# The reload of x for the residual, held behind the attention projection's sixth finished tile on GpSimd's own queue

## Chip, cores and metric

The kernel runs on one core of one Trainium2 chip. The metric is the device time of one execution in microseconds (us). "Median" is the median over the timed runs. The profile comes from one further execution; its span runs from the first to the last instruction, and its own device time is a little longer than its span.

## What is computed

One step of a hybrid decoder layer on 512 prompt tokens and 8 x 8 sample tokens (576 columns in all), with a model width of 1024. The part around the change is the end of the attention branch, the merge of the two branches by their gates, the output projection and the gated residual:

```python
mod = jax.nn.silu(c) @ w_ada + b_ada
sh1, sc1, g1, sh2, sc2, g2 = [m[:, None, :] for m in jnp.split(mod, 6, axis=-1)]
h = _rmsnorm(x, norm1_g) * (1.0 + sc1) + sh1
...
ya = (b_gate * uc) @ w_conv_out
...
yb = o @ w_attn_out
mixed = jax.nn.sigmoid(ga) * ya + jax.nn.sigmoid(gb) * yb
x = x + g1 * (mixed @ w_mix_out)
h2 = _rmsnorm(x, norm2_g) * (1.0 + sc2) + sh2
a, val = jnp.split(h2 @ w_up, 2, axis=-1)
```

After that come the FFN with its depthwise convolution, a second residual and a final norm.

## The kernel before

Activations are held transposed, as tiles of 128 features x 576 tokens; a matrix of width 1024 therefore is eight tiles (`NK = 8`). Every fp32 operand is split into a high and a low part (`split`, L136), and a product is three matmuls for each pair of tiles: high by high, high by low, low by high (`kstep`, L203; `product`, L215). ScalarE (ACT) makes the high parts, VectorE (DVE) the low parts. Some low parts of weights are made by a DMA that adds into its target, issued by GpSimd (POOL) in L175 and L408 (`wlo<-raw`, `wl<-s`).

SyncE (SP) issues nearly all loads: weight blocks of 512 KB into four buffers (`load_w`, L146, tile `raw`), columns of `w_ada` in pieces of 256 KB (L1234, tile `ada`), and the gates that had been parked in DRAM (`gate`, L1346, tile `gt`, 288 KB).

The modulation `mod` is made in the background. `modulation` (L1225) is a generator that loads 32 `ada` pieces and after every eight of them puts a group of 16 small matmuls on TensorE (PE), `side_by_side` (L1213, matmuls at L1218). `tick` (L188) pulls it along by a rate for each `kstep`. The last modulation (`modulations(1)`, L1472) runs beside the attention projection and gives the scale and gate of the FFN's norm and residual, so it has four such groups. What is left of it is run by `drain()` (L1522).

The loop at L1487 is the attention projection, `yb`. It goes through the eight output tiles in the order `turn = [0, 4, 1, 5, 2, 6, 3, 7]`; for the n-th tile it makes the product with `w_attn_out`, multiplies by the gate and adds `ya` (L1503, L1504). The result `t` is tile m = turn[n] of `mixed`, which is then split (L1513); for m >= 4, pair sums for the next product are made from it (L1521). The sixth finished tile is n = 5.

x had been written to a DRAM tensor `xT_dram` early in the kernel (L801). L1553 to L1556 read it back, as two transfers of 1152 KB on GpSimd's queue, into two buffers of the tag "oh", which held the attention output `ot` until then. The first reader is the residual after the first product with `w_mix_out` (L1590).

The order within each engine is set in two ways. Engines named in `pinned` keep the order of the program text; PE, ACT and DVE are pinned up to the fourth product of the loop (`pinned.clear()`, L1499) and again from L1589. Everything else is ordered by the compiler's planner, which runs a timeline of its own (`schedule_with_timeline_sim`, L2077). `tc.issue_after(i)` keeps the instructions traced inside its block behind instruction `i` where they are on the engine of `i`; it adds no wait between engines.

```python
        done = dve.tensor_tensor(out=t, in0=t, in1=ya[m], op=ALU.add)
        if n == 4:
            x1_after = done
...
    x1t = [wp.tile([P, 4, NT], F32, tag="oh", name=nm("x1"), bufs=2) for _ in range(2)]
    with tc.issue_after(x1_after.ins):
        for x in range(2):
            nc.gpsimd.dma_start(x1t[x], xT_dram[x])
```

Of the kernel before, what the change touches and what calls it, by code (L numbers as in the profile page):

```python
# [10 lines left out]
F32 = mybir.dt.float32  # L11
F32R = mybir.dt.float32r
AF = mybir.ActivationFunctionType
ALU = mybir.AluOpType
AX = mybir.AxisListType

P = 128
# [53 lines left out]
def step_kernel(ctx: ExitStack, tc: tile.TileContext, ins: dict, outs: list):  # L71
# [4 lines left out]
    cp = ctx.enter_context(tc.tile_pool(name="cp", bufs=1))  # L76
# [14 lines left out]
    def slot(s, dt=F32, shape=None):  # L91
        return ap_.tile(shape or [P, NT], dt, tag="a", name=nm(s))
# [22 lines left out]
    pe, act, dve, pool = (InOrder(e) for e in (nc.tensor, nc.scalar, nc.vector, nc.gpsimd))  # L115
# [11 lines left out]
    def sv(t):  # L127
        return t[:, 512:576]

    def b8(t):  # L130
        return t.rearrange("p (b t) -> p b t", b=8)
# [9 lines left out]
    def split_slot(src, s):  # L141
        hi, lo = slot(s + "h", F32R), slot(s + "l", F32R)
        split(hi, lo, src)
        return hi, lo

    def load_w(src, nk):  # L146

        raw = wp.tile([P, nk, P], F32, tag="raw", name=nm("raw"), bufs=W_BUFS)
        nc.sync.dma_start(raw, src)
        return raw  # L150

    def split_w(raw):
        nk = raw.shape[1]
        hi = wp.tile([P, nk, P], F32R, tag="whi", name=nm("whi"), bufs=S_BUFS)
        lo = wp.tile([P, nk, P], F32R, tag="wlo", name=nm("wlo"), bufs=S_BUFS)
        split(hi, lo, raw)
        return (lambda k: hi[:, k, :]), (lambda k: lo[:, k, :])
# [20 lines left out]
    def weights(src, nk):  # L178
        return split_w(load_w(src, nk))
# [35 lines left out]
    def product(w, xs):  # L215
        ps = mmps()
        for k in range(len(xs)):
            kstep(halves(ps), w, xs, k)
            tick()
        return pf(ps)  # L220
# [264 lines left out]
    def kpm(w, m0, k0=0, nk=NK):  # L485
        return w[k0 * P : (k0 + nk) * P, m0 : m0 + P].rearrange("(k p) m -> p k m", p=P)
# [316 lines left out]
    for j in (2, 0, 1):  # L803
        t = slot("kT")
# [5 lines left out]
    def state_load(src, n):  # L810
        parts = []
        for m0 in range(0, n, 4):
            c = min(4, n - m0)
            s = slot("st", shape=[P, 512])
            load(s[:16, : c * P], src.rearrange("o b r c -> (o b r) c")[:, m0 * P : (m0 + c) * P])
            parts.append(s)
        return parts
# [37 lines left out]
    for i in (3, 4):  # L855
# [3 lines left out]
        t = slot("kout", shape=[P, 256])  # L859
# [21 lines left out]
    def queries(t, ps=None):  # L881
# [52 lines left out]
        out=sel,  # L934
        in0=snk.rearrange("p (h g) -> p h g", h=4),
        in1=ind.unsqueeze(1).to_broadcast([P, 4, 4]),
        op=ALU.mult,
# [13 lines left out]
    def state_in(parts, nm_, n):  # L951
        t = cp.tile([P, n, 16], F32, tag=nm_, name=nm_)
        ps = aux()
        for m in range(n):
            c = m % 4 * P
            transpose(ps[:, m * 16 : m * 16 + 16], parts[m // 4][:16, c : c + P], ident[:16, :16])
        nc.scalar.copy(t.rearrange("p m r -> p (m r)"), ps[:, : n * 16])
        return t
# [211 lines left out]
    def b10(t):  # L1170
        return t[:, 514:594].rearrange("p (b e) -> p b e", b=8)
# [174 lines left out]
    def gate(x, m):  # L1346
        t = slot("gt")
        nc.sync.dma_start(t, sg_dram[x, m])
        return t

    ya, w_next, raw_ao, o, late = [], {}, {}, [], []
# [24 lines left out]
    for m in range(NK):  # L1376
# [29 lines left out]
        if m == NK - 1:  # L1406
# [10 lines left out]
            out=b10(u)[:, :, 2:10], in0=b8(sv(ps)), in1=b8(sv(c_sb)), op=ALU.mult  # L1417
# [69 lines left out]
    for n, m in enumerate(turn):  # L1487
        if n + 2 < NK:
            w_next[n + 2] = split_w(raw_ao.pop(n + 2))
        if n + 3 < NK:  # L1490
            raw_ao[n + 3] = load_w(kpm(wao, turn[n + 3] * P), NK)
        if n == NK - 2:
            w_mix0 = weights(kpm(wmx, 0), NK)
        ps = product(w_next.pop(n), o)
        if n == 0:
            for f in late[-2:]:
                f()
        if n == 3:
            pinned.clear()  # L1499
        t = gb.pop(m)  # L1500
        if n + 2 < NK:
            gb[turn[n + 2]] = gate(1, turn[n + 2])
        dve.tensor_tensor(out=t, in0=ps, in1=t, op=ALU.mult)  # L1503
        done = dve.tensor_tensor(out=t, in0=t, in1=ya[m], op=ALU.add)  # L1504
        if n == 4:
            x1_after = done
        if n == NK - 2:
            mix_jobs[0].load()
        if n == 3:
            st_ffn = state_load(ins["state_ffn_conv"], NF)  # L1510
        if n == 5:
            stF = state_in(st_ffn, "stF", NF)
        mixed[m], raw_mx[m] = split_slot(t, "mx"), t  # L1513
        if n == NK - 2:
            for fs in mix_jobs[0].prepare("BD").values():
                for f in fs:
                    f()
        if n == NK - 1:
            mix_jobs[1].load()
        if m >= 4:  # L1520
            BesideOperands(mixed[m - 4], mixed[m], raw_mx[m - 4], raw_mx[m], made_m).all()  # L1521
# [426 lines left out]
    for m0, m1 in FCH:  # L1948
# [29 lines left out]
        if m1 < NF:  # L1978
# [3 lines left out]
            n = m1 - m0  # L1982
# [51 lines left out]
        n = m1 - m0  # L2034
# [74 lines left out]
```

## Time and profile before

| what | us |
|---|---|
| median of 3 timed runs | 983.16 (982.19 to 985.09) |
| profiled execution, its own time | 985.19 |
| profiled execution, span | 983.4 |
| PE busy in the span | 966.2 |
| DVE busy | 687.1 |
| ACT busy | 520.5 |
| POOL busy | 126.4 |

The times of the trace below count from the start of the span. The attention projection runs from 460.4 us to about 526 us, the first product with `w_mix_out` follows. A row of the timeline gives start, duration, engine, line, operation, target and sources, and in square brackets the idle time of that engine just before it with what ended it. A row of the chain of waits gives start, duration and what the time was spent on. A row by stages (windows) gives the stretch, its length, the busy time of each engine with its number of instructions, the granted clock of PE as a share of full speed, the busy share of the 16 DMA engines and the GB/s that they moved. L110 is the line of the helper through which the pinned engines issue, so those groups are told apart by their tiles.

### The profile page before, as it was taken

The numbers are of one execution on the slowest core, as the hardware profiler recorded it, in microseconds if no ns is written. First come the engines' busy times: TensorE is split into PE (matmuls) and PEld (weight loads), VectorE is DVE, ScalarE is ACT, GpSimd is POOL, SyncE is SP. The second block draws the span as 40 slices with busy tenths as digits, with TensorE's granted clock in tenths as the row PEclk, the third lists the DMA queues.
The fourth block names the chain that finished last, engine by engine and source line by source line (L and its number), as shares of the span: only waits on it lengthen the run. The fifth ranks groups of instructions, "written<-read, shape, count | busy, mean of one in ns | idle before, by whom it ended". The sixth has DMA issues, their size and how long they took to land.

```text
span 983.4 us, 18791 instructions
## 1 busy us (share of the span) xinstructions
PE 966.2 (98%) x7396; PEld 926.6 (94%) x7396; DVE 687.1 (70%) x1284; ACT 520.5 (53%) x986; POOL 126.4 (13%) x308
## 2 busy tenths in 40 slices
PE   7999999999999999999899999999999999999997
PEld 5899999999999889999699999999999999999997
DVE  4747777677766567876576678995559974579664
ACT  4445666554655447875235557563236653246453
POOL 2222112111123002211001131000000000000020
PEclk8999999999999999999999999999999999999998
DMA  9984332233368867899883742232322332323212
GB/s 280 329 248 129 87 92 70 80 127 126 76 154 229 263 229 188 227 248 290 295 251 86 171 109 65 86 108 66 106 87 86 95 100 77 99 83 97 77 31 97
DMA packets 181531, 141.21 MB, mean 144 GB/s; under 512 B 7896, under 2 KB 161855, under 8 KB 181155
## 3 DMA queue, kind: packets, MB, share of 16 engines
q1 hardware_dynamic: 172258, 111.72, 37.3%
q0 software_dynamic: 9040, 28.03, 11.5%
q8 instruction: 58, 0.95, 0.4%
q14 instruction: 31, 0.25, 0.1%
q10 hardware_dynamic: 144, 0.26, 0.1%
HBM read 113.89 MB, written 12.07 MB: 128 GB/s over the span
## 4 chain that ended last, share of the span: by engine, by line
PE 94%; DMA 2%; issue 1%; ACT 1%; DVE 1%; SPq 0%; POOL 0%; POOLq 0%; DVEq 0%; ACTq 0%
PE mm L110 57%; PE aux L110 34%; PE aux L1218 2%; PE aux L1123 1%; DMA ada<-in_w_ada 1%; DMA x<-in_x_prompt 1%; SPq L491 0%; ACT junk L110 0%; ACT hh L110 0%; ACT whi L110 0%; POOL r L110 0%; DVE cs L498 0%; POOL rs L110 0%; DVE modT L110 0%; DVE hl L110 0%
## 5 line engine op out<-in xcount | busy, mean ns | idle before, releaser
L110 ACT ACTIVATE whi<-raw 128x1024 fp32r<-128x1024 f32 (+3 forms) x176 | 179.1, 1026 | 134.4 <-PE mm L110 69.7
L110 DVE TENSOR_TENSOR wlo<-raw,whi 128x1024 fp32r<-128x1024 f32 (+3 forms) x159 | 187.0, 1182 | 40.7 <-ACT whi L110 40.0
L110 PE MATMUL mm<-hh,whi 128*128 128x256 f32 (+1 forms) x400 | 88.5, 302 | 0.5 <-ACT hh L110 0.5
L110 PE MATMUL mm<-hh,wlo 128*128 128x256 f32 (+1 forms) x400 | 85.2, 294 | 0.0
L110 PE MATMUL mm<-hl,whi 128*128 128x256 f32 (+1 forms) x400 | 84.4, 295 | 0.1
L110 PE MATMUL aux<-2h,whi 128*128 128x288 f32 (+2 forms) x232 | 68.5, 295 | 0.0
L110 PE MATMUL aux<-2h,wlo 128*128 128x288 f32 (+2 forms) x232 | 68.4, 295 | 0.0
L110 PE MATMUL aux<-2l,whi 128*128 128x288 f32 (+2 forms) x232 | 68.3, 295 | 0.0
L110 PEld LDWEIGHTS mm<-hh,whi 128*128 128x128 f32 x400 | 65.5, 188 | 2.4 <-ACT hh L110 1.0
L110 PEld LDWEIGHTS mm<-hl,whi 128*128 128x128 f32 x400 | 66.2, 188 | 0.7 <-DVE hl L110 0.5
L110 PEld LDWEIGHTS mm<-hh,wlo 128*128 128x128 f32 x400 | 66.8, 188 | 0.0
L110 PE MATMUL mm<-fh,whi 128*128 128x256 f32 (+1 forms) x304 | 64.9, 295 | 0.3 <-DVE rt L110 0.3
L110 PE MATMUL mm<-fl,whi 128*128 128x256 f32 (+1 forms) x304 | 65.1, 296 | 0.0
L110 PE MATMUL mm<-fh,wlo 128*128 128x256 f32 (+1 forms) x304 | 65.0, 295 | 0.0
L110 DVE SCALAR_TENSOR_TENSOR x<-mm,modT,x 128x512 f32<-128x512 f32 (+2 forms) x31 | 20.6, 666 | 55.3 <-PE mm L110 55.2
L110 DVE TENSOR_TENSOR raw<-raw 128x512 f32<-128x512 f32 x72 | 50.5, 701 | 2.5
L110 PEld LDWEIGHTS mm<-fh,whi 128*128 128x128 f32 x304 | 50.6, 188 | 0.6 <-PE aux L110 0.6
L110 PEld LDWEIGHTS mm<-fh,wlo 128*128 128x128 f32 x304 | 51.0, 188 | 0.0
L110 PEld LDWEIGHTS mm<-fl,whi 128*128 128x128 f32 x304 | 50.7, 188 | 0.0
L110 PE MATMUL aux<-hh,whi 128*128 128x288 f32 (+2 forms) x160 | 46.5, 299 | 0.0
L110 PE MATMUL aux<-hl,whi 128*128 128x288 f32 (+2 forms) x160 | 45.9, 295 | 0.0
L110 PE MATMUL aux<-hh,wlo 128*128 128x288 f32 (+2 forms) x160 | 45.8, 295 | 0.0
(357 smaller groups left out, 2895.4 us busy)
## 6 DMA issues: line engine op xcount, KB each, us to landing
raw<-in_w_in SPq DMA_DIRECT2D x52, 512.0 KB, 5.1
raw<-in_w_up SPq DMA_DIRECT2D x44, 512.0 KB, 3.7
ada<-in_w_ada SPq DMA_DIRECT2D x64, 256.0 KB, 5.5
wlo<-raw POOLq DMA_DIRECT2D x17, 512.0 KB, 4.5
ad<-in_w_ada SPq DMA_DIRECT2D x32, 256.0 KB, 6.1
raw<-in_w_down SPq DMA_DIRECT2D x16, 512.0 KB, 3.9
sg_dram<-sg POOLq DMA_DIRECT2D x16, 288.0 KB, 5.1
gt<-sg_dram SPq DMA_DIRECT2D x16, 288.0 KB, 5.9
```

The lines of the kernel that those rows point to most:

```text
L110: done = getattr(self.engine, name)(*args, **kwargs)
L1123: done = nc.tensor.matmul(O[HALF[par], :256], vt(i - nkt + 1 + kt)[:, hd * 64 : hd * 64 + 64], pts[kt][:, par * 256 : par * 256 + 256], st ...
L1218: done = nc.tensor.matmul(ps[32 * j : 32 * j + 32, :], cT[:, k, :], cols[k][j], start=(k == 1), stop=(k == NK - 2),)
```

## The change

The reload is no longer held behind an instruction of DVE (the add of the fifth tile) but behind a new instruction of GpSimd: a copy of the first column of the sixth finished tile into a tile `mark` of 128 x 1. The copy itself waits for that tile's add on DVE. The two transfers of the reload are issued on the same queue as the copy, behind it.

```diff
         dve.tensor_tensor(out=t, in0=ps, in1=t, op=ALU.mult)
-        done = dve.tensor_tensor(out=t, in0=t, in1=ya[m], op=ALU.add)
-        if n == 4:
-            x1_after = done
+        dve.tensor_tensor(out=t, in0=t, in1=ya[m], op=ALU.add)
+        if n == 5:
+            mark = cp.tile([P, 1], F32, tag="mark", name="mark")
+            x1_after = pool.tensor_copy(out=mark, in_=t[:, 0:1])
         if n == NK - 2:
             mix_jobs[0].load()
```

## The prediction, made before the changed kernel was built or run

> **What bounds the kernel now.** I read the page first, then who waited for whom on PE, then the chain of waits around the projection, then the stages of that stretch.
>
> ```profile
> PE 966.2 (98%) x7396; PEld 926.6 (94%) x7396; DVE 687.1 (70%) x1284; ACT 520.5 (53%) x986; POOL 126.4 (13%) x308
> ...
> PE 94%; DMA 2%; issue 1%; ACT 1%; DVE 1%; SPq 0%; POOL 0%; POOLq 0%; DVEq 0%; ACTq 0%
> ```
>
> PE is the bound: of 983.4 us it idles for some 17. Only an edit that moves PE's idle time or PE's clock can move the end. PE's waits in the whole span, longest first:
>
> ```profile
> PE aux L110 <- POOL ident masks.py:199: 4.4, 1, 4.4
> PE aux L1218 <- DMA ada<-in_w_ada: 2.8, 1, 2.8
> PE aux L110 <- POOL rs L110: 1.9, 1, 1.9
> ```
>
> The largest is at the start, before anything here. The second is in the stretch of the change: a group of modulation matmuls (L1218) waits 2.8 us for an `ada` piece. The timeline and the chain of waits show it, and the other three groups beside it:
>
> ```profile
> 472.91 3.50 PE L1218 MATMUL aux<-ada,cT 128*32 128x512 f32 x16 [2.82 <-DMA ada<-in_w_ada]
> ...
> 460.40 12.46 DMA ada<-in_w_ada
> 472.87 0.04 issue
> 472.91 3.50 PE aux L1218 x16
> 476.41 12.97 PE mm L110 x96
> 489.38 1.85 PE aux L1218 x16
> 491.23 16.07 PE mm L110 x120
> 507.30 0.28 PE aux L110 x3
> 507.58 1.85 PE aux L1218 x16
> 509.44 1.28 PE aux L110 x19
> 510.72 10.51 PE mm L110 x78
> 521.23 1.85 PE aux L1218 x16
> ```
>
> The reader is to see two things. The piece was issued at 460.40 and landed 12.46 us later. And this group of 16 matmuls took 3.50 us, where the other three took 1.85. The stages give the reason for the second:
>
> ```profile
> 466.50:469.90 3.40, 3.40 (x28) 3.35 (x26) 1.64 (x3) 0.85 (x2) 0.00 (x0) 1.00 1.03 417
> 469.90:473.10 3.20, 0.38 (x6) 0.16 (x8) 1.85 (x2) 0.79 (x1) 0.00 (x0) 1.00 1.02 399
> 473.10:476.50 3.40, 3.40 (x17) 0.60 (x9) 0.00 (x0) 0.00 (x0) 0.00 (x0) 0.50 1.09 380
> 476.50:480.00 3.50, 3.50 (x27) 3.50 (x28) 0.10 (x1) 0.00 (x0) 0.00 (x0) 1.00 1.09 380
> ```
>
> After the stretch in which PE was busy for 0.38 of 3.20 us its granted clock was 0.50 for 3.4 us. All the while the DMA engines were busy without a break (share 1.02 to 1.09). So the wait costs 2.82 us and its echo in the clock 3.50 - 1.85 = 1.65 us: **4.47 us** in all.
>
> **What makes the piece late.** GpSimd's timeline shows the reload of x right there, and nothing else on that queue until 522.83:
>
> ```profile
> 459.67 0.55 POOL L1556 DMA_DIRECT2D x<-xT_dram  x1 [13.87 <-DVE ol L110]
> 463.38 0.54 POOL L1556 DMA_DIRECT2D x<-xT_dram  x1 [3.17 <-DVE ol L110]
> 522.83 0.88 POOL L110 DMA_DIRECT2D wl<-s  x1 [58.90 <-DVE raw L110]
> 525.97 0.87 POOL L110 DMA_DIRECT2D wlo<-raw  x1 [2.27 <-DVE wlo L110]
> ```
>
> It waits for the last split of the attention output (`ol`), which frees its buffers, and for nothing later: the fifth tile's add, behind which the program text puts it, comes at 503.0 (row below). So the hold of before does nothing. How the queues share the engines between 464 and 472 (q0 is GpSimd's, q1 SyncE's), and how long an `ada` piece took that was issued at 458.8, ahead of the reload:
>
> ```profile
> DMA packets 868, 3.23 MB, mean 404 GB/s; under 512 B 95, under 2 KB 95, under 8 KB 643
> ...
> q0 software_dynamic: 256, 2.07, 63.0%
> q1 hardware_dynamic: 612, 1.16, 38.4%
> ...
> DMA to landing us min/median/max: 6.1/6.1/6.1
> ```
>
> The reload took 2.07 of 3.23 MB; SyncE's queue was left 1.16 MB in 8 us, 0.145 MB/us, where all engines together move 0.404. The piece issued at 458.8, into the same crowd of SyncE's loads, landed in 6.1 us.
>
> **The change part by part.**
>
> 1. *The reload leaves 460 to 472.* By the 6.1 us the piece of 460.40 lands at 466.5. PE asks for it at 472.91 - 2.82 = 470.09. That leaves 3.6 us of room. At the late end it lands where it does now. I take the first: the wait goes, and with it the stretch of half clock. Minus 4.47 us. Everything behind it on PE comes 4.47 us earlier; below I keep the times of before, since the later steps hang on PE's products and move along.
>
> 2. *The copy.* No copy of one column is in the trace; the nearest row is a copy of two:
>
> ```profile
> L1195 POOL COPY sto<-pad x30: 184/185/1244, 88.1 to 928.9; 128x2 f32<-128x2 f32 x30
> ...
> L110 DVE TENSOR_TENSOR gt<-gt,ya x2: 753/756/760, 503.0 to 508.1; 128x576 f32<-128x576 f32 x2
> ```
>
> 0.18 us, at the worst 1.2. Those two adds are the fifth and the sixth tile's; the sixth ends at 508.1 + 0.76 = 508.9. The copy lies on POOL, which is idle from 463.9 to 522.8, and delays only the reload. Cost on the path: 0. Behind the waiting copy stand the two transfers and then `wl<-s` at 522.83, which has 12 us of room after the reload's issue.
>
> 3. *The reload's two issues* (0.55 and 0.54 us) move from 459.67 and 463.38 to about 509.1 and 509.7, no longer 3.7 us apart. Who needs them is the first residual on DVE:
>
> ```profile
> 532.47 0.75 DVE L110 SCALAR_TENSOR_TENSOR x<-mm,modT,x 128x512 f32<-128x512 f32 x1 [1.06 <-PE mm L110]
> ...
> x<-xT_dram POOLq DMA_DIRECT2D x2, 1152.0 KB, 9.4
> ```
>
> With 9.4 us the transfers land at 518.5 and 519.1; with 12.5, the longest landing seen beside it, at 522.2. Both are 10 us ahead of 532.47. If that cover were gone, every us late would be one on the path.
>
> 4. *What the reload now meets.* SyncE's last loads and the DMA engines behind them:
>
> ```profile
> 508.59 1.77 SPq L1234 DMA_DIRECT2D ada<-in_w_ada  x4
> 510.45 0.38 SPq L1348 DMA_DIRECT2D gt<-sg_dram  x1
> 510.93 0.38 SPq L1234 DMA_DIRECT2D ada<-in_w_ada  x1
> 526.01 17.32 SPq L149 DMA_DIRECT2D raw<-in_w_mix_out  x3
> ...
> q1 hardware_dynamic: 672, 1.24, 71.2%
> ...
> 512.00:516.00 4.00, 4.00 (x32) 4.00 (x32) 1.49 (x2) 0.69 (x1) 0.00 (x0) 1.00 0.70 236
> 516.00:524.00 8.00, 8.00 (x63) 6.40 (x62) 4.95 (x7) 3.60 (x6) 0.88 (x1) 1.00 0.00 1
> ```
>
> From 516 to 524 the engines are idle, which is room for most of the reload. In front of that, between 511 and 516.2, SyncE's queue moves its last 1.24 MB (the q1 row), and the last of it is the `ada` piece issued at 510.93, which the fourth group needs at 521.23. At the shared rate of 0.145 MB/us those 1.24 MB take 8.6 us and end at 519.6: in time. At the other end the piece takes 12.46 us, as its sister did beside the reload: 523.4, a wait of 2.2 us. Nearer is the first, since the gate ahead of it and the idle 516 to 524 leave it more room; I take 0.3 us for it, with 0 and 2.2 as ends.
>
> Sum: -4.47 + 0 + 0.3 = **-4.17 us** on a span of 983.4 and a profiled time of 985.19: 981.0 for such an execution. That one was 2.03 above the median of 983.16; on the median the sum gives **979.0 us**.
>
> **The rivals.**
>
> *The clock does not echo in the timed runs.* The half clock is seen in one execution. If in most of the others a gap of 2.82 us passes without it, only the gap is to be had: 983.16 - 2.82 = 980.3. For it: the timed runs spread by 2.9 us, and 985.19 is the slowest of all. Against: in the one trace there is, the gap did it. The Trainium skill (TensorE: Matmul & The Clock Gate, "Why this matters for your kernels") asks for no idle gaps above some 3 us, and by that a gap of 2.82 should be harmless; this trace disagrees, with a clock of 0.50 after it. The same page, in its Part 1, says that the windows in which activity is counted run free of the kernel, so that it can differ between executions; no run here shows that yet.
>
> *The wait moves to the fourth group.* Its last piece lands at 523.4 as worked out above: 2.2 us of wait, and with the echo 1.65 more. Of 4.47 us 0.6 are left: 982.5. For it: the same two queues, the same kind of load. Against: the DMA engines have nothing else to do from 516 on, where at 460 to 480 they were full.
>
> *The fourth group is put earlier (slower).* From the fifth product on PE's order is the planner's, and a timeline in which the reload sits elsewhere can put the group at the end of the seventh product, 510.72 + 48 x 10.51 / 78 = 517.2. With its piece at 523.4 it would wait 6.2 us, and 1.65 for the clock: 7.85 - 4.47 = +3.4, 986.5. It decides against the change from a landing of about 520 on, 2.8 us behind the group's place. Against: the piece's own issue hangs on the products too, and the planner sees the reload as well.
>
> *Nothing is held.* Should the reload still go out at 460, the time stays 983.2. For it: the hold of before had no effect. Against: copy and transfers now share a queue, and a copy that reads the sixth tile can't run before 508.9.
>
> **How the numbers follow.** Forecast 0.57, echo absent 0.13, fourth group waits 0.12, nothing held 0.05, slower 0.13. A change of 0.3%, 2.95 us, is about what this measurement can tell from none, so faster means below 980.2. The forecast lies below it but for 0.01; the rival of the echo straddles it, half on each side: faster 0.56 + 0.06 = 0.62. The fourth group's wait and the hold without effect count as same, with the rest of the other two: 0.12 + 0.05 + 0.01 + 0.07 = 0.25. Slower 0.13. The range starts at the full 4.47 off the median with the scatter of the fastest timed run (983.16 - 982.19 = 0.97): 977.7. It ends at 983.4, past the hold without effect, and leaves out the slower case and little else. The forecast's own range is 977.7 to 980.2.
>
> **What would show it.** Right: the reload's two issues on POOL just behind a copy near 505 (508.9 less the 4.47); the first group of L1218 without idle time before it, all four groups at about 1.85 us, no 0.50 in the clock near 473; the fourth group with less than 1 us of wait; the residual on DVE released by PE and not by the transfer. Wrong: a wait of the first group that stays with the reload gone (then SyncE's own loads made it late), a fourth group that waits for `ada` over 2 us, or another order of SyncE's loads with a wait of PE for weights that is not there now.

## The result and the profile after

| | before | after |
|---|---|---|
| median, us | 983.31 (22 runs, 981.29 to 985.09) | 982.19 (22 runs, 981.21 to 983.58) |
| profiled execution, span | 983.4 | 979.8 |
| profiled execution, own time | 985.19 | 981.58 |

The ratio is 0.9990, with a 95% interval of 0.9983 to 0.9996: some 1.0 us faster, where 4.2 were forecast. The one profile shows 3.6 us. That difference is what has to be explained.

First the profile. Who waited for whom on PE, and the chain of waits around the projection, both of after:

```profile
PE aux L110 <- POOL ident masks.py:199: 4.4, 1, 4.4
PE aux L110 <- POOL rs L110: 1.6, 1, 1.6
PE aux L110 <- ACT row L1241: 0.7, 1, 0.7
```

```profile
459.09 11.26 PE mm L110 x84
470.35 1.85 PE aux L1218 x16
472.20 12.88 PE mm L110 x96
485.09 1.85 PE aux L1218 x16
486.94 16.07 PE mm L110 x120
503.01 0.28 PE aux L110 x3
503.30 1.85 PE aux L1218 x16
505.15 1.28 PE aux L110 x19
506.43 12.88 PE mm L110 x96
519.31 1.92 PE aux L1218 x16
521.23 0.02 issue
521.26 0.59 ACT row L1241
521.85 0.04 issue
521.90 0.66 PE aux L110 x4
522.55 6.37 PE mm L110 x48
```

The wait of 2.8 us for `ada` is gone and the first group takes 1.85 us in place of 3.50. The fourth group has moved: before, it stood inside the eighth product, with 18 matmuls of that product behind it, now it stands behind the whole product. So the copy of its row (ACT, L1241), which the transposes need, is no longer covered by matmuls: a new wait of 0.7 us.

GpSimd's timeline of after, the landing of the two transfers (least, median, most, in us) and the first residual on DVE:

```profile
504.66 0.19 POOL L110 COPY mark<-gt 128x1 f32<-128x1 f32 x1 [58.63 <-DVE gt L110]
505.17 1.10 POOL L1557 DMA_DIRECT2D x<-xT_dram  x2 [0.32 <-issue]
518.52 0.88 POOL L110 DMA_DIRECT2D wl<-s  x1 [12.25 <-DVE raw L110]
```

```profile
DMA to landing us min/median/max: 8.8/10.2/11.7
```

```profile
528.96 0.75 DVE L110 SCALAR_TENSOR_TENSOR x<-mm,modT,x 128x512 f32<-128x512 f32 x1 [2.40 <-PE mm L110]
```

The hold works: copy at 504.66, both transfers behind it, landed by about 518 (505.7 + 11.7 at the latest), 11 us ahead of the residual, which is released by PE.

The last `ada` piece of the fourth group does meet the reload in its new place. Its issue on SyncE's queue, and its landing:

```profile
506.62 0.42 SPq L1234 DMA_DIRECT2D ada<-in_w_ada  x1
```

```profile
DMA to landing us min/median/max: 11.5/11.5/11.5
```

It landed at 518.1, so the group at 519.31 found it there with 1.2 us to spare. At the group's old place, 18 matmuls before the end of the product (2.4 us by the 96 in 12.88 us), PE would by this estimate have asked for it at 516.9 and waited 1.2 us.

### The profile page after: what moved, and what is told of

Read it like the earlier page. It is cut to its first block, busy times and chain, and to the rows that moved or that the text cites. A ratio compares the mean times of both kernels' runs of the same rounds, so it can differ in the third digit from the quotient of the medians.

```text
span 979.8 us, 18792 instructions
## 1 busy us (share of the span) xinstructions
PE 965.0 (98%) x7396; PEld 926.0 (95%) x7396; DVE 687.9 (70%) x1284; ACT 520.9 (53%) x986; POOL 128.0 (13%) x309
## 4 chain that ended last, share of the span: by engine, by line
PE 94%; DMA 2%; issue 1%; SPq 0%; DVE 0%; ACT 0%; POOL 0%; POOLq 0%; DVEq 0%
PE mm L110 58%; PE aux L110 34%; PE aux L1218 2%; PE aux L1123 1%; DMA ad<-in_w_ada 1%; DMA raw<-in_w_in 1%; SPq L491 0%; ACT whi L110 0%; ACT wlo L110 0%; POOL r L110 0%; DVE cs L498 0%; ACT hh L110 0%; DVE hl L110 0%; DVE x L110 0%; DVE yo L110 0%
## 5 line engine op out<-in xcount | busy, mean ns | idle before, releaser
L110 PEld LDWEIGHTS mm<-hh,whi 128*128 128x128 f32 x400 | 65.5, 188 | 2.4 <-ACT hh L110 1.1
```

The lines of the kernel that those rows point to most:

```text
L110: done = getattr(self.engine, name)(*args, **kwargs)
```

## The experiments

**More executions of both kernels.** Two kernels, unchanged, each profiled twice more. Theory A is that the wait differs from one execution to the next and that the profile of before was an extreme one; theory B, that the 4.47 us are in every execution of before and that after loses them elsewhere.

> The kernel before, unchanged, profiled once more. Theory A (the wait of the first modulation group differs from one execution to the next, and the profiled execution of before was an extreme one): a wait between 0 and 2.8 us, the half clock behind it not always there, and an own time that is lower than 985.19 by about what is missing of the 4.47 us. Theory B (the 4.47 us are in every execution of before, and the timed runs of after lose about 3 us somewhere that its one profile does not show): a wait of 2.5 us or more with the half clock, and an own time of 983 to 985.

> As the run before it, a further execution. Theory A: another wait than in the run before, by half a us or more. Theory B: the same wait within 0.3 us.

> The kernel after, unchanged, profiled once more. Theory A: no wait of the first group, a wait of 0.7 us for the row copy as in the first profile, own time 981 to 983.5, with the difference between executions outside the attention projection. Theory B: a wait of 2 us or more somewhere that the first profile of after does not have, own time around 982.2 or above.

> As the run before it, a further execution. Theory A: again no wait of the first group, 0.7 us for the row copy. Theory B: a wait of 2 us or more that the first profile does not have.

PE's timeline in the two further executions of before: the first matmul of the projection, the first group of L1218, and the first matmul of the product behind the projection; behind each, the stage that follows the wait (its third number from the end is the granted clock):

```profile
459.70 0.42 PE L110 MATMUL mm<-oh,whi 128*128 128x256 f32 x2
...
472.34 2.48 PE L1218 MATMUL aux<-ada,cT 128*32 128x512 f32 x16 [2.99 <-DMA ada<-in_w_ada]
...
525.18 0.51 PE L110 MATMUL mm<-mxh,whi 128*128 128x256 f32 x2
```

```profile
473.60:477.00 3.40, 3.40 (x17) 2.25 (x10) 0.00 (x0) 0.00 (x0) 0.00 (x0) 0.50 1.10 387
```

```profile
458.80 0.42 PE L110 MATMUL mm<-oh,whi 128*128 128x256 f32 x2
...
470.72 1.92 PE L1218 MATMUL aux<-ada,cT 128*32 128x512 f32 x16 [2.26 <-DMA ada<-in_w_ada]
...
521.99 0.51 PE L110 MATMUL mm<-mxh,whi 128*128 128x256 f32 x2
```

```profile
470.70:474.10 3.40, 3.38 (x27) 1.94 (x28) 0.40 (x1) 0.00 (x0) 0.00 (x0) 1.00 1.09 382
```

And the third group in the two further executions of after:

```profile
503.77 1.92 PE L1218 MATMUL aux<-ada,cT 128*32 128x512 f32 x16 [0.49 <-DMA ada<-in_w_ada]
```

```profile
504.76 1.92 PE L1218 MATMUL aux<-ada,cT 128*32 128x512 f32 x16 [1.41 <-DMA ada<-in_w_ada]
```

Own times: before 984.54 and 981.31, after 982.11 and 983.09. Both theories are half right. The wait itself is there each time (2.82, 2.99 and 2.26; mean 2.69), so B holds for the wait. Its echo is not: 3.4 us of half clock follow in the first two executions of before and none in the third, so A holds for that. From the first matmul of the projection to the first one behind it the two took 525.18 - 459.70 = 65.5 and 521.99 - 458.80 = 63.2 us: 2.3 us apart, 0.7 of it wait and 1.6 echo. (In the first of them the half clock begins 1.3 us into the group and slows the next product as well; the group's own 2.48 us show only part of it.) The 4.47 us were one kind of execution; the mean of three is 2.69 + 2/3 x 1.65 = 3.8. And after has a wait that its first profile did not show, on the third group, of 0, 0.49 and 1.41 us.

One thing more differed in all six, far from the change. The stage from 15 to 30 us, where the loads run without a break, in before and in after (the last three columns are granted clock, DMA share, GB/s):

```profile
15.00:30.00 15.00, 13.18 (x107) 9.04 (x108) 9.12 (x21) 5.47 (x14) 2.25 (x5) 0.77 1.10 368
```

```profile
15.00:30.00 15.00, 13.58 (x108) 8.46 (x109) 8.83 (x18) 5.38 (x13) 1.97 (x5) 0.89 1.10 347
```

The share is the same, the rate is not: 368, 370 and 369 GB/s in the three executions of before, 347 in all three of after. PE, DVE, GpSimd and SyncE run the same instructions there in the same order. Nor does the rate follow PE's clock, which differs here as well: 368 GB/s at 0.77 and 370 at 1.00 in before, 347 at 0.89 and at 1.00 in after. In the records of single packets of 512 bytes on SyncE's queue between 12 and 60 us the median duration is 27 ns before and 31 ns after; the packets of 1024 bytes, which carry nine tenths of the bytes between 15 and 30 us, take 47.6 and 50.2 ns in the mean. What did change is where tiles lie: in the built program `mark` takes 32 bytes of each partition, and every tile placed behind it lies 32 bytes further on. The weight buffers (`raw`) begin at 151040 in before, a multiple of 256, and at 151072 in after.

**The tile apart from the hold.** Theory C: the move by 32 bytes makes the loads slower and eats part of the gain. Rival D: the rates differ by chance, and the third group waits because PE now comes earlier. In the first kernel the copy goes into a tile that exists already and is free by then; the second is before, with the tile alone.

```diff
-            mark = cp.tile([P, 1], F32, tag="mark", name="mark")
-            x1_after = pool.tensor_copy(out=mark, in_=t[:, 0:1])
+            x1_after = pool.tensor_copy(out=first, in_=t[:, 0:1])
```

> The change without its new tile: the copy of the column goes into the tile 'first' of L494, which is not used any more by then, so no tile moves; the order of every engine is that of after. Theory C (the tile 'mark' moves all tiles that were placed behind it by 32 bytes, which makes loads slower: this eats part of the gain): DMA rate between 15 and 30 us as in before (365 to 375 GB/s, not 340 to 355), projection from 458.8 to 460.4 instead of 460.7, no wait of the third group, 0.7 us for the row copy as in after, median 2.0 to 3.0 us below before. Rival D (the rates at the start differ by chance, and the third group waits because PE comes earlier): as after, 1.0 us below before, third group waits between 0 and 1.4 us.

```diff
         if n == 4:
             x1_after = done
+        if n == 5:
+            mark = cp.tile([P, 1], F32, tag="mark", name="mark")
+            pool.memset(mark, 0.0)
```

> The kernel before with the tile 'mark' alone, set to zero by GpSimd; the reload stays where it was, the order of the other engines is that of before. Theory C: DMA rate between 15 and 30 us of 340 to 355 GB/s, median 0.7 to 1.7 us above before. Rival D: within 0.3 us of before, rate 365 to 375 GB/s.

Without the tile: 980.58 against 982.56 us, ratio 0.9977 (0.9968 to 0.9986). The tile alone: 985.24, ratio 1.0024 (1.0015 to 1.0034). The same stage, without the tile and with the tile alone:

```profile
15.00:30.00 15.00, 13.64 (x120) 9.31 (x121) 9.60 (x22) 5.57 (x14) 2.18 (x6) 1.00 1.10 369
```

```profile
15.00:30.00 15.00, 13.26 (x110) 8.05 (x111) 8.87 (x18) 5.47 (x13) 2.00 (x5) 1.00 1.10 346
```

The rate goes with the tile and not with the hold, and so does the time; D falls as far as the rates go. A tile with four bytes in each partition that nothing reads costs the kernel before 2.4 us; the mechanism of the change, without its tile, is worth 2.3. Between after and the kernel without the tile lie 0.9990 - 0.9977, or 1.3 us.

In the kernel with the tile alone the first group waits as in before, with its echo (2.01 us, and 3.23 in place of 1.85, in the second row below), and there is a wait at 84 us that no other profile has:

```profile
84.38 0.36 PE L110 MATMUL aux<-kh,q 128*128 128x256 f32 x1 [1.30 <-DMA q<-low]
...
473.79 3.23 PE L1218 MATMUL aux<-ada,cT 128*32 128x512 f32 x16 [2.01 <-DMA ada<-in_w_ada]
```

Whether that wait comes with the tile is not shown: it stands in one execution, and none of the five profiles of the change with a tile that slows the loads has it. So the 2.4 us are less sure as a price of the loads alone than the 1.3.

The traces show where the change loses the 1.3 us. The first matmul of the projection without the tile and in after:

```profile
459.03 0.42 PE L110 MATMUL mm<-oh,whi 128*128 128x256 f32 x2
```

```profile
460.68 0.42 PE L110 MATMUL mm<-oh,whi 128*128 128x256 f32 x2
```

Over all profiles of the change here and below (but for the last kernel, whose order differs), it starts at 459.0, 460.4 and 459.4 us with the loads at their full rate and at 460.7, 460.7, 460.7, 460.4 and 460.0 with the slower ones: 0.9 us later in the mean, though the two sets overlap. PE's records stand in the same order in these eight traces, and by the 301st matmul, at 44 us, the 0.9 us are there; they don't grow up to the projection. The waits of the third group add 0.5 us in the mean. So the slower loads cost time at the start of the kernel and, it may be, at the third group, and not all along.

**Which move costs.** The change with larger tiles, all else as in after; `raw` then begins 64, 128 or 256 bytes further on than in before.

```diff
-            mark = cp.tile([P, 1], F32, tag="mark", name="mark")
-            x1_after = pool.tensor_copy(out=mark, in_=t[:, 0:1])
+            mark = cp.tile([P, 16], F32, tag="mark", name="mark")
+            x1_after = pool.tensor_copy(out=mark[:, 0:1], in_=t[:, 0:1])
```

> The change with a tile of 64 bytes instead of 4 (which takes 32): the tiles behind it move by 64 bytes. Theory C, with a boundary of 64 bytes that counts: as without the tile, 2.0 to 3.0 us below before. Theory C with a boundary of 256 bytes that counts, as the Trainium skill has it for descriptors (DMA: Bandwidth & Descriptors, 'How a descriptor splits into AXI transactions'): as after, about 1.0 us below before, rate 340 to 355 GB/s between 15 and 30 us. Rival D: as after.

> The change with a tile of 128 bytes: the weight buffers, which begin on a multiple of 256 bytes in before, begin 128 bytes off. If a boundary of 128 bytes is enough for the loads: as the run without the tile, ratio about 0.9977, 368 GB/s between 15 and 30 us. If it takes 256: as after, ratio about 0.999, 347 GB/s.

> The change with a tile of 256 bytes: all tiles behind it move, but the weight buffers begin on a multiple of 256 bytes again. If it is the offset from a boundary of 256 bytes that makes the loads slower: as the run without the tile, ratio about 0.9977, 368 to 370 GB/s between 15 and 30 us, projection at about 459. If it is any move, or the tile's own work: as after, ratio about 0.999, 347 GB/s, projection at 460.7.

| bytes that the tile takes | ratio to before | GB/s, 15 to 30 us | wait of the third group, us (each execution so far) |
|---|---|---|---|
| 0 | 0.9977 (0.9968 to 0.9986) | 369 | 0.57 |
| 32 (after) | 0.9990 (0.9983 to 0.9996) | 347 | 0, 0.49, 1.41 |
| 64 | 0.9991 (0.9981 to 1.0000) | 347 | 0.49 |
| 128 | 0.9989 (0.9979 to 0.9999) | 347 | 0.85 |
| 256 | 0.9972 (0.9961 to 0.9983) | 369 | 0 |

The stage in the kernels of 64, 128 and 256 bytes, in this order:

```profile
15.00:30.00 15.00, 13.86 (x112) 8.29 (x113) 8.54 (x17) 5.48 (x13) 1.46 (x5) 1.00 1.10 347
```

```profile
15.00:30.00 15.00, 13.68 (x114) 8.99 (x115) 8.83 (x18) 5.38 (x13) 1.96 (x5) 0.89 1.11 347
```

```profile
15.00:30.00 15.00, 13.62 (x117) 9.53 (x118) 9.51 (x21) 5.37 (x13) 2.24 (x5) 0.89 1.10 369
```

A move by 256 bytes costs nothing, although all tiles behind it have moved; each of the three smaller ones costs the same 6% of the rate. So it is the offset from a boundary of 256 bytes (a boundary of 512 is not needed: 151040 is a multiple of 512 too, and 256 bytes further on is not). The Trainium skill (DMA: Bandwidth & Descriptors, "How a descriptor splits into AXI transactions") has descriptors cut into pieces that begin on such a boundary, by which 512 bytes off the boundary need three pieces in place of two; the boundary agrees with these runs, and that 32, 64 and 128 bytes cost alike fits a price for each piece. But the packets of 512 bytes take 15% longer and not half as long again, so the extra piece, if it is one, costs less than a whole one. The page speaks of reads, where these runs move the place that is written, so this mechanism is not shown.

> The change without the tile, one more execution. If the wait of the third group belongs to the slower loads: no wait here. If it belongs to PE coming 4 us earlier: again some tenths of a us up to 1.4. The row copy 0.7 us as before.

That execution of the kernel without the tile has no wait of the third group, at 981.34 us. With `raw` on the boundary the third group waited 0.57, 0 and 0 us (two executions without the tile, one of 256 bytes), off it 0, 0.49, 1.41, 0.49 and 0.85. Both reasons may have a part; these few executions don't divide it.

**The row copy covered again.** What is left of the modulation runs behind the first product with `w_mix_out`, in the kernel without the tile:

```diff
-    drain()
...
-    affine(A2, 32, 56, NK)
...
     residual(product(w_mix0, mixed), x1[0], 16)
+    drain()
+    affine(A2, 32, 56, NK)
```

> The change without its tile, and with what is left of the modulation run behind the first product with w_mix_out instead of ahead of it (drain and the scale made from it, L1522 and L1552, moved behind L1590): the fourth group stays at the end of the projection, but six matmuls lie between it and the transposes of its row. If the 0.7 us for the row copy are worth what the trace says: 0.7 us below the run without the tile, and no wait for the row copy. If that wait is hidden anyway: the same as that run.

979.72 against 982.56 us, ratio 0.9971 (0.9960 to 0.9983). PE's timeline there:

```profile
518.12 1.92 PE L1218 MATMUL aux<-ada,cT 128*32 128x512 f32 x16
...
520.88 0.60 PE L110 MATMUL aux<-ident,row 128*128 128x128 f32 x4
```

The transposes no longer wait (0.73 us before them in after). The medians differ by 0.86 us from the kernel without the tile, near the 0.7 expected, though the intervals of the two ratios overlap. This kernel's one profile has no wait of the third group either, so the 0.86 us need not all be the row copy. Its loads moved 355 GB/s between 15 and 30 us at a DMA share of 1.06 (367 at 1.10 up to 20 us): the engines were less busy there, not slower. It is the fastest kernel of the study, some 2.8 us below before.

## Why the prediction was wrong

*What bounds the kernel, and the late piece.* Right, and by its mechanism: with the reload held, the first group has no wait in any of the nine profiled executions that hold it.

*Part 1, "minus 4.47 us", on the median.* Over-sized. 2.82 us is near the mean of 2.69; the echo of 1.65 was there in two of three profiled executions. The profiled execution of before was, at 985.19, slower than each of the 22 timed ones, and the prediction noted that it lay 2.03 above the median; it then took that execution's whole sum off the median. By three executions that is 0.7 us of the miss (4.47 - 3.8). The rival of the absent echo had this mechanism, but as all or nothing.

*"Everything behind it on PE comes 4.47 us earlier."* Wrong for the third group, which the prediction did not look at: in its profile of before the group's last piece was issued at 501.60 and landed 5.5 us later, at 507.1, for a use at 507.58. That was half a us of room (2.1 and 2.3 us in the two further executions). In after the piece is issued between 496.3 and 498.1 and lands 6.0 to 6.6 us later, and PE, which comes at 503.3 in place of 507.58, meets it: up to 1.4 us of wait.

*Part 2, "cost on the path: 0".* The copy costs nothing (0.19 us on an idle engine). **The tile that it writes was not costed at all**, and it was the step that failed most plainly: 32 bytes in front of the weight buffers take 6% off the rate of the loads and cost 1.3 us of 983.

*Part 3.* Right: the issues stand behind the copy, and the reload lands 11 us ahead of the residual.

*Part 4, "I take 0.3 us for it".* The fourth group does not wait for `ada`, but not for the reason given, and so by luck. The prediction put its piece's landing nearer to the early end; in the nine executions with the held reload it took 10.5 to 12.0 us, close to the 12.46 of the late end, and as worked out above it would have cost 1.2 us in after had the group stayed. The planner moved that group, as the slower rival had it, but later and not earlier; why it did is not shown. The price was 0.73 us for the row copy, which no rival named.

The sum as the runs have it: 3.8 us removed by the three profiles; 0.73 given back to the row copy; some 0.2 to the third group (mean of 0.57, 0 and 0). That makes 2.9, and the kernel without the tile measures 2.3 (1.4 to 3.1); the three profiled executions of before have a mean of 983.7, 0.4 above the median of the 22. The tile takes 1.3 us of the 2.3. What is left is 1.0, the measured gain.

## What to carry to other kernels

A tile added for synchronisation alone is not free: see where it moves the buffers that DMAs write, and put it into a tile that exists, or let it take a multiple of 256 bytes. Where a profile's own time lies at the edge of the timed runs, take its waits off that time and not off the median, and profile a few more executions before a wait of 3 us is priced with its echo in the clock. When a wait on PE goes, look at the next loads on the same queue: what had half a us to 2 us of room can be the next wait.

## What the runs showed of the hardware

A target that lies 32, 64 or 128 bytes off a boundary of 256 takes these loads, nearly all in packets of 512 and 1024 bytes, from 369 to 347 GB/s, while the engines show the same busy share of 1.10. A busy share doesn't tell that a transfer has become dearer; the rate beside it does.

A gap of PE of 2 to 3 us may or may not halve the clock for 3.4 us, which costs some 1.6: gaps of 2.82, 2.99 and, in the kernel with the tile alone, 2.01 us did, one of 2.26 did not. That a shorter gap did and a longer one did not fits the statement of the Trainium skill (TensorE: Matmul & The Clock Gate, Part 1) that the windows in which activity is counted run free of the kernel; the limit of some 3 us that the same page sets ("Why this matters for your kernels") was not low enough here.
